# A quarter of the weights' low parts on GpSimd, in the mixers of the second block

## The chip, the cores and the metric

The kernel runs on one core of one Trainium2 chip. The metric is device time in microseconds, from the start of the program to its end. The engines are named as in the profile: PE is TensorE (PEld its weight loads), DVE is VectorE, ACT is ScalarE, POOL is GpSimd, SP is SyncE, whose queue issues the loads of weights.

## The reference

A sequence of 256 positions with 1024 features goes through two blocks. The first has four layers (attention of three kinds, each followed by a SwiGLU feed-forward). The second, where the change lies, has two layers of this form:

```
h = rmsnorm(x, attn_norm_g[layer])
proj = h @ w_in[layer]
gm_u, gm_v, ssm_z, ssm_xbc, ssm_dt, da_q, da_k, da_v, gates = split_cols(proj, IN_SIZES)
y_a = chunked_spatial_gating(gelu(gm_u), gelu(gm_v), ...)
y_b = mamba2_mixer(ssm_z, ssm_xbc, ssm_dt, ...)
y_c = diff_attention(da_q, da_k, da_v, ...)
g = sigmoid(gates).reshape(bsz, s, N_BRANCH, D_MODEL)
merged = (g[:, :, 0] * (y_a @ w_branch_a[layer]) + g[:, :, 1] * (y_b @ w_branch_b[layer])
          + g[:, :, 2] * (y_c @ w_branch_c[layer]))
x = x + merged @ w_out[layer]
h = rmsnorm(x, ffn_norm_g[layer])
up = causal_dwconv(h @ ffn_w_up[layer], ffn_conv_w[layer], ffn_conv_b[layer])
gate, val = split(up, 2, axis=-1)
x = x + (silu(gate) * val) @ ffn_w_down[layer]
```

The part up to `merged @ w_out` is the mixer. All of it is in float32.

## The kernel before

**Products in three parts.** A float32 product with weights is made from high and low parts. An operand is split into a high part (a cast to fp32r) and a low part (the operand minus its high part), and `mm3` adds three matmuls in one PSUM bank: high by high (L394), high by low weight (L395), low by high weight (L396). The sequence is two tiles of 128 positions, t = 0 and t = 1, each of which uses every weight.

**Weights in units and halves.** `plan` lists all weights as units in the order in which tile t = 0 uses them: first-block units, then, from `units_1` on, those of the second block. A unit is 4 rows of 128 by 512 columns, or 2 rows by 1024. It is loaded in two halves; half a of unit n has the number 2n + a. `load` makes a half: SP's queue loads it into a raw buffer (four of them, `wr`), ScalarE casts the high part into a buffer `w` (seven of them in the second block, `wh`) at L382, and then two subtractions of 128x512 (L385), one for each half of the columns, make the low part from the raw buffer and the high part. The raw buffer comes free when the second subtraction has ended, the `w` buffer when the matmuls of both tiles have read it. `get` asks for a half when tile t = 0 needs it and for one half ahead (`AHEAD = 1`).

**Who makes low parts.** The set `self.aside`, filled in `run`, holds the numbers of the halves whose low part GpSimd makes; VectorE makes all others. `part` gives every unit a kind: 0 for a mixer and 1 for a feed-forward of the first block, 2 for a mixer and 3 for a feed-forward of the second. Before the change the set holds 11 halves, just behind changes from one part to the next in the first block (`BOUND`); none lie in the second block.

**What sets the order.** The code issues the work of the two tiles in turns, tile t = 1 four turns behind (`LAG`), with tasks spawned for the convolution (L985 on VectorE, history copies L976 and L979 on GpSimd), state space (`ssm`, L1033 to L1104), differential attention (`diff_attn`), gates and merges (L1318 to L1325). The Tile framework then lays the order of the instructions of each engine when the kernel is built, after its own estimate of their durations, so that the matmuls of the two tiles interleave; each engine runs its own queue strictly in that order. Tiles named `pj`, `ch` and `tp` are PSUM banks, and so are the `accs` of L526 (`layer_norm`); all others lie in SBUF. Small loads, such as gains, are DMAs on GpSimd's queue (L494).

Of the kernel before, what the change touches and what calls it, by code (L numbers as in the profile page):

```python
# [82 lines left out]
class Net:  # L83
# [1338 lines left out]
    def run(self):  # L1422
        self.units = self.plan()
        self.index = {u[0]: n for n, u in enumerate(self.units)}

        self.aside = set()
        part = [2 * (n >= self.units_1) + ("ff" in str(u[0])) for n, u in enumerate(self.units)]
        for n in range(1, len(part)):
            if part[n - 1] != part[n]:
                self.aside |= {2 * n + a for a in BOUND[part[n]]}  # L1430
        self.loaded = 0
        self.tiles = {}
        self.cache = {}
        self.tasks = [[], []]
        self.x = []
        self.load_x()
        self.streams = [self.stream(0), self.stream(1)]
        self.live = [True, True]
        if not self.first:
            self.passed = 2  # L1440

        self.late = bool(self.first) and self.first[0] % 3 == 0
        n = 0
        while any(self.live):
            if self.live[0]:
                self.turn(0)
            if n == TABLES:
                self.tables()
                if not self.late:
                    for _ in self.more_tables():  # L1450
                        pass
            if self.live[1] and (n >= LAG or not self.live[0]):
                self.turn(1)
            n += 1
        self.phase.close()
# [29 lines left out]
```

## Time and profile before

| | us |
|---|---|
| median of 3 runs | 2401.51 (2400.18 to 2401.63) |
| the profiled execution | 2397.69 |
| its span, first to last instruction | 2395.8 |
| TensorE busy | 2358.1 |
| VectorE busy | 1739.8 |
| ScalarE busy | 1320.2 |
| GpSimd busy | 148.1 |

The granted TensorE clock is 0.999 of full speed over the span. In the profile's rows a time is in microseconds unless marked ns; L385 is line 385 of the kernel; `w<-raw,w` says what an instruction writes and reads; "xN" is a count. The first layer's mixer of the second block runs from about 1420 to 1700 us, the second layer's from about 1915 to 2195.

### The profile page before, as it was taken

The page shows a single profiled execution, that of the slowest core. Times are in us where ns is not written, and L with a number is a line of the kernel's source. Part 1 is how long each engine was busy: PE and PEld are TensorE (multiplying, and loading weights), DVE is VectorE, ACT ScalarE, POOL GpSimd, SP SyncE. Part 2 cuts the span into 40 slices and gives each one's busy share as a digit, 9 for nine tenths or more (in the row PEclk, how much of TensorE's full clock was granted, in tenths as well). Part 3 has the DMA queues.
Part 4 walks back from the last instruction along what each step waited for, and adds up shares of the span by engine and source line. Part 5 has one row for each costly group of instructions (what it writes and reads, how often), then busy time and mean ns, then how long its engine had stood idle before and what let it go on. Part 6 is the DMA issues. An engine that isn't in the chain of part 4 may idle for free.

```text
span 2395.8 us, 35093 instructions
## 1 busy us (share of the span) xinstructions
PE 2358.1 (98%) x11720; PEld 1926.0 (80%) x11720; DVE 1739.8 (73%) x4255; ACT 1320.2 (55%) x2182; POOL 148.1 (6%) x428
## 2 busy tenths in 40 slices
PE   8999999999999999999999999999999999999999
PEld 6788878888788788887778878887888788888887
DVE  7755576666755767557775588987877889987876
ACT  6544456555444555444544445744577656545776
POOL 1100000000100001000010000100011201000111
PEclk9999999999999999999999999999999999999999
DMA  6366654444566545665365657567565686575653
GB/s 233 106 189 189 185 167 132 133 132 131 171 189 187 185 132 167 187 188 184 124 182 190 186 140 168 136 147 198 165 194 184 166 187 132 123 213 172 189 184 115
DMA packets 280117, 400.16 MB, mean 167 GB/s; under 512 B 20588, under 2 KB 205098, under 8 KB 279936
## 3 DMA queue, kind: packets, MB, share of 16 engines
q1 hardware_dynamic: 274784, 381.88, 54.8%
q0 software_dynamic: 5152, 16.05, 2.2%
q8 instruction: 92, 1.51, 0.3%
q14 instruction: 89, 0.73, 0.1%
HBM read 396.81 MB, written 1.05 MB: 166 GB/s over the span
## 4 chain that ended last, share of the span: by engine, by line
PE 87%; DVE 8%; DMA 3%; ACT 2%; issue 1%; SPq 0%; ACTq 0%; DVEq 0%
PE pj L394 21%; PE pj L396 21%; PE pj L395 21%; PE tp L439 4%; PE ch L394 4%; PE ch L396 4%; PE ch L395 4%; PE ch L596 3%; PE ch L634 2%; DVE w L385 2%; DMA raw<-in_w_in_dram 2%; PE tp L646 1%; ACT w L382 1%; DMA raw<-in_a_w_qkv_dram 1%; DVE convy L985 1%
## 5 line engine op out<-in xcount | busy, mean ns | idle before, releaser
L385 DVE TENSOR_TENSOR w<-raw,w 128x512 fp32r<-128x512 f32 x1434 | 942.9, 684 | 469.3 <-ACT w L382 468.2
L382 ACT CAST w<-raw 128x1024 fp32r<-128x1024 f32 x728 | 758.5, 1043 | 661.2 <-PE pj L396 370.9
L394 PE MATMUL pj<-w,xth 128*128 128x512 f32 x2048 | 820.4, 401 | 7.1 <-ACT xth L432 6.8
L395 PE MATMUL pj<-w,xth 128*128 128x512 f32 x2048 | 803.3, 393 | 1.1 <-DVE w L385 1.1
L396 PE MATMUL pj<-w,xtl 128*128 128x512 f32 x2048 | 802.4, 393 | 1.8 <-DVE xtl L433 1.8
L394 PEld LDWEIGHTS pj<-w,xth 128*128 128x128 f32 x2048 | 385.5, 188 | 90.8 <-ACT xth L432 12.4
L396 PEld LDWEIGHTS pj<-w,xtl 128*128 128x128 f32 x2048 | 385.0, 188 | 86.4 <-DVE xtl L433 5.0
L395 PEld LDWEIGHTS pj<-w,xth 128*128 128x128 f32 x2048 | 386.0, 188 | 76.8 <-DVE w L385 2.0
L394 PE MATMUL ch<-w,fht 128*128 128x512 f32 x412 | 171.4, 416 | 1.8 <-ACT fht L432 1.8
L396 PE MATMUL ch<-w,fht 128*128 128x512 f32 x412 | 161.4, 392 | 0.0
L395 PE MATMUL ch<-w,fht 128*128 128x512 f32 x412 | 160.9, 391 | 0.0
L985 DVE SCALAR_TENSOR_TENSOR convy<-xc,ffn_cw,convy 128x128 f32<-128x128 f32 x352 | 100.7, 347 | 7.1 <-POOL ffn_hist L976 2.1
L396 PEld LDWEIGHTS ch<-w,fht 128*128 128x128 f32 x412 | 77.3, 188 | 17.9 <-DVE fht L433 1.0
L394 PEld LDWEIGHTS ch<-w,fht 128*128 128x128 f32 x412 | 77.5, 188 | 15.4 <-ACT fht L432 3.9
L395 PEld LDWEIGHTS ch<-w,fht 128*128 128x128 f32 x412 | 77.9, 189 | 11.9
L623 ACT ACTIVATE pexp<-ch,nm 128x128 f32<-128x128 f32 (+1 forms) x192 | 65.6, 421 | 33.8 <-DVE nm L618 24.0
L827 ACT ACTIVATE ffg<-pj 128x256 f32<-128x256 f32 x88 | 33.8, 384 | 86.2 <-PE pj L396 86.2
L982 ACT ACTIVATE convy<-xc,ffn_cw 128x128 f32<-128x128 f32 x176 | 72.8, 484 | 1.4
L634 PEld LDWEIGHTS ch<-v,pt 128*128 128x128 f32 x576 | 70.6, 192 | 2.9
L394 PE MATMUL pj<-w,fht 128*128 128x512 f32 x180 | 71.3, 396 | 0.0
L396 PE MATMUL pj<-w,fht 128*128 128x512 f32 x180 | 70.7, 393 | 0.0
L395 PE MATMUL pj<-w,fht 128*128 128x512 f32 x180 | 70.2, 390 | 0.0
(333 smaller groups left out, 2758.8 us busy)
## 6 DMA issues: line engine op xcount, KB each, us to landing
raw<-in_w_gate_up_dram SPq DMA_DIRECT2D x352, 256.0 KB, 3.2
raw<-in_w_in_dram SPq DMA_DIRECT2D x128, 512.0 KB, 5.1
raw<-in_w_down_dram SPq DMA_DIRECT2D x88, 512.0 KB, 3.6
raw<-in_ffn_w_up_dram SPq DMA_DIRECT2D x176, 256.0 KB, 3.3
raw<-in_b_w_qkv_dram SPq DMA_DIRECT2D x144, 256.0 KB, 3.1
raw<-in_ffn_w_down_dram SPq DMA_DIRECT2D x44, 512.0 KB, 4.4
raw<-in_a_w_qkv_dram SPq DMA_DIRECT2D x24, 512.0 KB, 4.4
raw<-in_c_w_qkv_dram SPq DMA_DIRECT2D x48, 256.0 KB, 3.2
```

The source lines that it names most:

```text
L382: nc.scalar.copy(w[:, 0, :m], raw)
L385: e.tensor_sub(w[:, 1, s], raw[:, s], w[:, 0, s].bitcast(F32))
L394: mm(ps, xh[:, k, :], wh[:, kk, cols], start=start, stop=False)
L395: mm(ps, xh[:, k, :], wl[:, kk, cols], start=False, stop=False)
L396: mm(ps, xl[:, k, :], wh[:, kk, cols], start=False, stop=stop)
L439: self.nc.tensor.transpose(tp[:, b * P:(b + 1) * P], src[:, b * P:(b + 1) * P], self.ident)
L596: nc.tensor.matmul(svs[par][:, a, j * P:(j + 1) * P], q(par, a), k(par, a, j), start=True, stop=True)
L623: nc.scalar.activation(p[:, a, :(t + 1) * P], sv[:, a, :], AF.Exp, bias=n2[:, a:a + 1])
L634: nc.tensor.matmul(o[:, par + 2 * a, :], pts[par][:, a * (t + 1) + j, :], v(j, par + 2 * a), start=j == 0, stop=j == t)
L827: nc.scalar.activation(g, ps[:, :FFC], AF.Silu)
L982: nc.scalar.activation(y[:, a, :], xc[:, a, 4:], AF.Identity, bias=b[:, 0, c:c + 1], scale=w[:, h, c:c + 1])
L985: nc.vector.scalar_tensor_tensor(y[:, a, :], xc[:, a, o:o + P], w[:, j, c:c + 1], y[:, a, :], op0=OP.mult, op1=OP.add)
```

## The change

One statement is added in `run`: in the mixers of the second block (kind 2), the first half of each unit with an even number goes into the set of halves whose low part GpSimd makes. Each mixer has 45 units, from number 208 and from number 286, so these are 46 halves of 180. Each is two subtractions of 128x512. The unit of the time steps (`dt`, 16 columns) has an odd number and stays as it is. Nothing else in the code changes: `load` picks the engine, `e`, by the set.

```
--- before.py
+++ after.py
@@ -1428,6 +1428,8 @@
         for n in range(1, len(part)):
             if part[n - 1] != part[n]:
                 self.aside |= {2 * n + a for a in BOUND[part[n]]}
+
+        self.aside |= {2 * n for n in range(len(part)) if part[n] == 2 and n % 2 == 0}
         self.loaded = 0
         self.tiles = {}
         self.cache = {}
```

## Rows read from the trace of the kernel before

**Rows 1.** The page, first part: busy time, share of the span, instructions.

```profile
PE 2358.1 (98%) x11720; PEld 1926.0 (80%) x11720; DVE 1739.8 (73%) x4255; ACT 1320.2 (55%) x2182; POOL 148.1 (6%) x428
```

**Rows 2.** Table by stretches: length; busy PE, PEld, DVE, ACT, POOL; clock, DMA share, GB/s.

```profile
1480.00:1550.00 70.00, 69.82 (x395) 57.27 (x392) 67.02 (x211) 49.63 (x104) 8.70 (x26) 1.00 0.59 144
1550.00:1645.00 95.00, 93.35 (x481) 76.53 (x479) 83.40 (x205) 44.29 (x63) 1.74 (x4) 1.00 0.65 152
...
1980.00:2045.00 65.00, 64.75 (x364) 53.51 (x364) 61.28 (x199) 46.58 (x95) 10.88 (x27) 1.00 0.57 128
2045.00:2140.00 95.00, 94.53 (x490) 78.53 (x489) 85.23 (x201) 45.05 (x62) 1.09 (x2) 1.00 0.67 160
...
sum 543.00, PE 537.65 PEld 441.13 DVE 462.23 ACT 295.58 POOL 25.66; mean PE 67.21 PEld 55.14 DVE 57.78 ACT 36.95 POOL 3.21
```

**Rows 3.** Waits of PE, 1426 to 1700: releaser, us in total, times, longest.

```profile
PE pj L394 <- DVE sg L1318: 1.5, 1, 1.5
PE pj L395 <- DVE w L385: 1.1, 1, 1.1
```

**Rows 4.** Waits of SP's DMA queue, 1426 to 1700.

```profile
SPq L374 <- DVE w L385: 244.4, 84, 8.7
```

**Rows 5.** Groups, count, busy us and mean ns: VectorE 1420 to 1700, GpSimd whole.

```profile
L385 DVE TENSOR_TENSOR w<-raw,w 128x512 fp32r<-128x512 f32 (+1 forms) x169 | 110.4, 673 | 20.6 <-ACT w L382 20.4
...
L385 POOL TENSOR_TENSOR w<-raw,w 128x512 fp32r<-128x512 f32 x22 | 28.6, 1319 | 556.8 <-ACT w L382 547.0 <-DVE eg L789 9.8
```

**Rows 6.** Timeline, ACT and DVE near 1668: start, us, instruction, [idle before].

```profile
1667.41 1.05 ACT L382 CAST w<-raw 128x1024 fp32r<-128x1024 f32 x1 [1.67 <-issue]
...
1668.76 1.29 DVE L385 TENSOR_TENSOR w<-raw,w 128x512 fp32r<-128x512 f32 x2
```

**Rows 7.** Timeline, POOL's subtractions near 923 and 1111 and DVE under them.

```profile
923.34 2.60 POOL L385 TENSOR_TENSOR w<-raw,w 128x512 fp32r<-128x512 f32 x2 [1.04 <-ACT w L382]
...
923.49 1.24 DVE L473 SCALAR_TENSOR_TENSOR rs_a<-rs_y,bnve 128x1 f32<-128x1 f32 x1
...
1111.68 2.56 POOL L385 TENSOR_TENSOR w<-raw,w 128x512 fp32r<-128x512 f32 x2 [164.41 <-ACT w L382]
...
1111.86 0.69 DVE L526 SCALAR_TENSOR_TENSOR x<-x,ch 128x512 f32<-128x512 f32 x1 [0.46 <-PE ch L396]
```

**Rows 8.** Lines 473 and 477: duration ns min/median/max, first and last start.

```profile
L473 DVE SCALAR_TENSOR_TENSOR rs_a<-rs_y,bnve x48: 182/213/1254, 104.4 to 1418.7; 128x1 f32<-128x1 f32 x48
...
L477 DVE SCALAR_TENSOR_TENSOR rs_y<-rs_a,rs_y x96: 143/158/1219, 104.9 to 2020.9; 128x1 f32<-128x1 f32 x60, 128x8 f32<-128x8 f32 x24, 128x4 f32<-128x4 f32 x12
```

**Rows 9.** Timeline of DVE: first and last of fourteen lengthened instructions.

```profile
106.13 0.73 DVE L477 SCALAR_TENSOR_TENSOR rs_y<-rs_a,rs_y 128x1 f32<-128x1 f32 x1
...
1211.79 1.00 DVE L473 SCALAR_TENSOR_TENSOR rs_a<-rs_y,bnve 128x1 f32<-128x1 f32 x1
```

**Rows 10.** Groups of DVE, 1420 to 1700: the convolution.

```profile
L985 DVE SCALAR_TENSOR_TENSOR convy<-xc,ssm_cw,convy 128x128 f32<-128x128 f32 x72 | 20.1, 347 | 0.6 <-issue 0.5
```

**Rows 11.** Timeline, ACT, DVE and PE, 1552 to 1566: one half's cast, subtraction, use.

```profile
1552.42 1.05 ACT L382 CAST w<-raw 128x1024 fp32r<-128x1024 f32 x1
...
1554.83 2.71 DVE L985 SCALAR_TENSOR_TENSOR convy<-xc,ssm_cw,convy 128x128 f32<-128x128 f32 x10
...
1565.05 0.68 DVE L385 TENSOR_TENSOR w<-raw,w 128x512 fp32r<-128x512 f32 x1
...
1565.95 0.40 PE L395 MATMUL pj<-w,xth 128*128 128x512 f32 x1
```

**Rows 12.** Timeline, ACT and PE, 1635 to 1639: a half's cast and first use.

```profile
1635.27 1.05 ACT L382 CAST w<-raw 128x1024 fp32r<-128x1024 f32 x1 [2.31 <-PE tp L439]
...
1638.19 0.48 PE L394 MATMUL pj<-w,xth 128*128 128x512 f32 x1
```

**Rows 13.** Timeline of POOL, 1545 to 1604.

```profile
1545.67 2.13 POOL L979 COPY xc<-ssm_hist 128x3 f32<-128x3 f32 x4 [4.68 <-DVE spa L1000]
...
1603.38 0.56 POOL L494 DMA_DIRECT2D sng<-in_ssm_norm_g_dram  x1 [51.31 <-DVE ssl L1085]
```

More of the change, by code (lines that the diff above doesn't have):

```diff
@@ L1430, in run @@
                 self.aside |= {2 * n + a for a in BOUND[part[n]]}
+        self.aside |= {2 * n for n in range(len(part)) if part[n] == 2 and n % 2 == 0}
         self.loaded = 0
```

## The prediction

> **What bounds the kernel now.** I read the page first: TensorE is busy 98% of the span, VectorE 73%, ScalarE 55%, GpSimd 6% [rows 1]. An edit that takes work from VectorE can therefore win only where TensorE waits for it. The edit acts in the two mixers of the second block, so the second view was the table by stretches: in the 543 us from 1426 to 1700 and from 1926 to 2195, TensorE is busy 537.65 us and VectorE 462.23 us (85%), by the last row, which sums all eight stretches [rows 2]. TensorE stands still for only 543 - 537.65 = 5.4 us there; since a matmul's end is modelled, some more waiting hides in lengthened matmuls. The stages are unlike. In the four stretches 1480:1550, 1550:1645, 1980:2045 and 2045:2140 (convolution, state space, attention; 325 us, "dense" below) VectorE is idle 3.0 + 11.6 + 3.7 + 9.8 = 28 us; in the other four it is idle 543 - 462 - 28 = 53 of 218 us. The view of waits names what TensorE waits for in the first mixer: the low part of a weight (1.1 us) and the merge of a branch (1.5 us), both VectorE's [rows 3]. VectorE also holds up the loads: the DMA queue waits 244.4 of 274 us for a low part, because the subtraction is the last reader of a raw buffer, and there are four of those [rows 4]. So the edit has a point; the question is what GpSimd's work does to VectorE.
>
> **The change part by part.** Each mixer has 45 units and starts at an even unit number (208 and 286), so even units are 23 in each: 46 first halves, two subtractions each, 92 instructions move.
>
> *Off VectorE.* One subtraction lasts 0.67 us [rows 5], but two in a row take 1.29 us together, so each occupies the engine 1.29 - 0.69 = 0.60 us [rows 6]. 92 x 0.60 = 55 us come off the 462.
>
> *Onto GpSimd.* The 22 that it makes now last 1.319 us each [rows 5]: 92 x 1.32 = 121 us on an engine that is busy 25.7 us in those 543 [rows 2]. It does not become a bound.
>
> *What GpSimd's instruction costs VectorE.* This decides the sign. Under GpSimd's subtractions at 923.34, VectorE's little L473 takes 1.24 us [rows 7], where its group's median is 0.213 [rows 8]; it ends when the first subtraction ends. Under those at 1111.68, VectorE's L526 of 128x512 takes its plain 0.69 us [rows 7]. The difference is where the inputs lie: L473 reads two tensors from SBUF, L526 reads one from SBUF and one from PSUM (accs). I went through all of VectorE's instructions that overlap one of the 22: fourteen are longer than the median of their group, from L477 at 106.13 to L473 at 1211.79 [rows 9], all fourteen read two SBUF tensors, and together they are 9.35 us longer. That is 9.35 / 22 = 0.42 us of lost VectorE time per GpSimd subtraction, the lower bound; the upper bound is its whole duration, 1.32 us. The Trainium skill (SBUF — State Buffer, section "Who interferes with whom") says that a VectorE instruction with two SBUF inputs contends with a GpSimd instruction that reads SBUF, and that whoever comes first at the shared ports keeps them for its whole instruction while the other stands still. By that rule alone, with VectorE always at the port, the whole 1.32 us would be lost each time, which the second rival prices; the trace agrees with the mechanism and shows a third of that price so far.
>
> Where those 22 ran, VectorE was mostly in a layer norm on PSUM operands or waiting. The mixers differ: the subtractions themselves and the convolution's L985 make up 110.4 + 20.1 us of VectorE's time in one mixer, which is about 462 / 2 = 231 [rows 2, 5, 10], and they read two SBUF tensors each, as do the norms, gates and rope. So I went to the end of each of the 46 casts, where GpSimd could start, left out the half's own two subtractions, and read how much of its 1.25 us is left when VectorE next begins an instruction with two SBUF inputs. One example of each kind: the cast that starts at 1552.42 ends at 1553.47 amid the convolution, whose ten L985 follow in one run of 2.71 us, so both subtractions would block in full [rows 11]; the one that starts at 1667.41 ends at 1668.46, and VectorE's next work is the very two subtractions that leave it, so next to nothing is blocked [rows 6]. The sum over the 46 is 57 us, 0.62 each, between the bounds. I take it. Over both mixers VectorE thus gains 55 and loses 57: nothing. But it is split unevenly: in the dense stretches 22 halves free 44 x 0.60 = 26 us and block 34 us, a net loss of 8 us; the quiet ones gain 6 us where VectorE idles anyway, worth nothing.
>
> *From VectorE to TensorE.* In the dense stretches TensorE follows VectorE closely: the low part finished by the subtraction that starts at 1565.05 is read at 1565.95 [rows 11]. Of the 8 us I let half through, since VectorE still has 28 us of idle time there: +4 us (bounds 0 and 8).
>
> *What the moved halves gain.* They leave VectorE's queue. The half cast by 1553.47 gets its low part begun only at 1565.05 [rows 11]; GpSimd would have it done near 1556.5, and its raw buffer would be free that much earlier, for one load in four. That can shorten the two waits of [rows 3]: I take -1.5 us in all (bounds 0 and -5.4, TensorE's idle time).
>
> *Is GpSimd too slow?* It needs 0.08 + 2 x 1.3 = 2.6 us from the cast's end to the second piece. The moved half with the least time is cast from 1635.27 to 1636.32 and first used at 1638.19 [rows 12], with its second piece due at 1639.2, 2.9 us after the cast. One lock wait would make it late by under 1 us. The other 45 have 2.8 to 18 us. I take 0 (bounds 0 and 2).
>
> *Other queues.* No DMA is added; SP's loads keep their order. On GpSimd's queue the subtractions stand among copies of the convolution's history, which start VectorE's convolution [rows 13], and DMAs of gains that wait for a free slot. A copy behind a pair of subtractions comes up to 2.6 us late; covered by VectorE's backlog, taken as 0 (bounds 0 and 3). The Tile framework also lays a new order of instructions on all engines when the kernel is built; nothing in the trace prices that, and I allow 3 us to either side, about the sum of the two waits of [rows 3].
>
> Sum: 4 - 1.5 = +2.5 us. The profiled execution took 2397.7 us (2395.8 of span), so 2400.2 by it; the runs shown have a median of 2401.5, 3.8 more, so 2404.
>
> **The rivals.**
> *VectorE is relieved (faster).* If the block stays at the 0.42 us of [rows 9], the dense stretches gain 44 x (0.60 - 0.42) = 8 us of VectorE time, and the loads run ahead. TensorE then gets back its 5.4 us of idle time and a little of what hides in lengthened matmuls: about -7, 2394.5. For it speaks that VectorE holds the loads [rows 4]; against it, that the mixers hold far more two-input work than the places of the 22.
> *The lock takes VectorE (slower).* In the dense stretches VectorE always has another two-input instruction next. At 1.0 us per subtraction it loses 44 x 0.40 = 18 us there, and of its 28 idle us many are waits for TensorE's scores and products, so two thirds go through: +12, 2413.5. At the whole 1.32 us it would be 32 us lost, past all idle time, and about +20. It decides from about 0.85 us per instruction, where the loss in the dense stretches passes 11 us and about 5 of it gets through. For it: the convolution run in [rows 11]. Against: 0.78 is what the reading gives for the dense stretches.
> *A stopped GpSimd queue (slower).* The gain's DMA at 1603.38 sat 51.31 us waiting for VectorE to free its slot [rows 13]. Were the half cast by 1553.47 queued behind it, its low part, due at 1565.95, would come some 38 us late: 2440. It needs Tile to have ordered the two the wrong way round.
> *It does less than it says.* If gain and loss both fall into slack, the time stays 2401.5; that lies within the forecast.
>
> **How the numbers follow.** The forecast, no change that can be told, has 0.41, and by itself 2397 to 2406.5; relief 0.24; the lock 0.31; the stopped queue 0.04. A measurement of this kernel can tell about 0.2% (4.8 us) from no change, so faster is 0.24, same 0.41, slower 0.35. The range takes in the relief and the lock at 1.0 us with 1 us around each: 2393 to 2415; outside it are the stopped queue, the lock at its full price and a gain beyond TensorE's idle time.
>
> **What would show it.** Right: 92 more GpSimd subtractions of 1.25 to 1.6 us, VectorE's two-input instructions under them lengthened by about 0.6 us each, VectorE's busy time in the mixers about where it was, TensorE's busy share there within a percent. Relief: TensorE's idle time in the dense stretches near zero and the DMA queue's wait for low parts clearly below 244 us. The lock: VectorE's dense stretches above 95%, and new waits of TensorE for low parts, scores and merges. Wrong altogether: TensorE waiting for GpSimd's own low parts for more than 2 us, or a change of time outside the two mixers.

## The result

The changed kernel takes 2426.28 us (median of 5 runs, 2424.43 to 2428.62) against 2401.51: the ratio is 1.0108, interval 1.0096 to 1.0119. It is slower by 24.8 us, outside the predicted range and on the side to which I gave 0.35. The profiled execution took 2425.71 us, 2424.0 of it span, 28.2 more than before.

The first part of the page of the changed kernel (busy time, share of the span, instructions) answers to [rows 1]:

```profile
PE 2365.8 (98%) x11720; PEld 1929.3 (80%) x11720; DVE 1742.9 (72%) x4163; ACT 1319.7 (54%) x2182; POOL 271.1 (11%) x520
```

GpSimd has its 92 subtractions more. VectorE has 92 fewer and yet is busy 3.1 us longer: what it was relieved of it lost again, as predicted. The table by stretches, columns as in [rows 2], shows where the time went (the work stands some microseconds later than before in the same stretch):

```profile
1480.00:1550.00 70.00, 64.93 (x355) 52.06 (x356) 64.02 (x184) 40.10 (x88) 16.64 (x26) 0.98 0.51 115
1550.00:1645.00 95.00, 88.65 (x465) 72.35 (x464) 88.32 (x203) 48.25 (x74) 23.07 (x23) 1.00 0.63 148
...
1980.00:2045.00 65.00, 60.08 (x325) 47.99 (x324) 59.78 (x176) 38.12 (x80) 14.98 (x22) 1.00 0.57 121
2045.00:2140.00 95.00, 90.60 (x479) 75.17 (x478) 84.78 (x207) 49.94 (x80) 22.47 (x30) 0.96 0.59 145
...
sum 543.00, PE 520.51 PEld 423.89 DVE 453.60 ACT 284.15 POOL 132.53; mean PE 65.06 PEld 52.99 DVE 56.70 ACT 35.52 POOL 16.57
```

In the four dense stretches TensorE stood still 0.2 + 1.7 + 0.2 + 0.5 = 2.6 us before [rows 2]; now it is 5.1 + 6.4 + 4.9 + 4.4 = 20.7 us. VectorE's idle time in the same stretches is 6.0 + 6.7 + 5.2 + 10.2 = 28.1 us, and it was 28 before. So TensorE waits more while VectorE has no less to spare: no engine is full, and what is lost is lost in waits of one engine for another.

Waits of PE in the changed kernel (releaser: us in total, times, longest), first from 1426 to 1700, where [rows 3] stood, then from 1980 to 2140, where two waits of 0.3 and 0.2 us stood:

```profile
PE tp L439 <- DVE stg L566: 4.0, 2, 3.0
PE tp L439 <- DVE convy L1227: 2.6, 1, 2.6
PE pj L395 <- DVE w L385: 2.1, 2, 1.4
PE tp L646 <- DVE dap L1137: 1.2, 2, 0.7
...
PE ch L1043 <- DVE ssda L1033: 3.4, 1, 3.4
PE tp L646 <- DVE dap L1137: 2.6, 3, 1.7
PE tp L439 <- DVE rs_a L476: 2.2, 1, 2.2
```

Hardly any of it is for low parts (2.1 us). TensorE waits for the ends of VectorE's chains: the norm and rope of queries and keys (L476, L566), the convolution (L1227), the attention's softmax (L1137), softplus (L1033). The first of these can be followed instruction by instruction. The timeline of the changed kernel, GpSimd, VectorE and TensorE:

```profile
1476.56 2.56 POOL L385 TENSOR_TENSOR w<-raw,w 128x512 fp32r<-128x512 f32 x2 [3.27 <-ACT w L382]
...
1476.53 1.35 DVE L476 TENSOR_TENSOR rs_a<-rs_a,rs_y 128x8 f32<-128x8 f32 x2
...
1477.87 1.35 DVE L477 SCALAR_TENSOR_TENSOR rs_y<-rs_a,rs_y 128x8 f32<-128x8 f32 x2
...
1482.48 0.28 DVE L566 TENSOR_TENSOR stg<-ropea,ropeb 128x128 f32<-128x128 f32 x1
...
1482.91 0.63 PE L439 MATMUL tp<-ident,stg 128*128 128x128 f32 x4 [3.04 <-DVE stg L566]
```

and the same two pairs of instructions in the kernel before:

```profile
1473.27 0.28 DVE L476 TENSOR_TENSOR rs_a<-rs_a,rs_y 128x8 f32<-128x8 f32 x2
...
1473.54 0.24 DVE L477 SCALAR_TENSOR_TENSOR rs_y<-rs_a,rs_y 128x8 f32<-128x8 f32 x2
```

Each row is a pair, and in each pair one tiny VectorE instruction is held until one of GpSimd's two subtractions ends: 1.35 instead of 0.28 us, 1.35 instead of 0.24. These are links of the chain that ends at L566, and TensorE, which runs its queue strictly in order, stands 3.04 us in front of the transpose that reads it. In the kernel before it stood 0.78 us in front of these transposes already:

```profile
1478.03 0.63 PE L439 MATMUL tp<-ident,stg 128*128 128x128 f32 x4 [0.78 <-DVE stg L566]
```

The two holds, 1.07 and 1.11 us, are about the rest. A stop of that length costs a second time. The table by stretches around it (the third figure from the right is the granted clock):

```profile
1479.00:1483.00 4.00, 0.96 (x5) 0.49 (x4) 4.00 (x17) 0.88 (x2) 0.12 (x1) 1.00 0.59 189
1483.00:1487.00 4.00, 4.00 (x20) 2.92 (x21) 2.63 (x8) 0.73 (x2) 0.00 (x0) 0.58 0.27 77
1487.00:1491.00 4.00, 4.00 (x21) 3.13 (x20) 3.34 (x12) 4.00 (x13) 0.00 (x0) 0.99 0.17 61
```

After TensorE stood nearly still for 3 us, the granted clock is 0.58 over the next 4 us, so for most of them at the lower level of 1.2 GHz, the 1.7 us that 0.42 x 4 makes. Over the page TensorE's busy time is 7.7 us longer, 2365.8 after 2358.1; the other 20 of the 28 us are standing still.

Two rows on the moved work itself: the group of GpSimd's subtractions, with the 22 old ones (answers to [rows 5]), and the waits of SP's queue from 1426 to 1700 (answers to [rows 4]):

```profile
L385 POOL TENSOR_TENSOR w<-raw,w 128x512 fp32r<-128x512 f32 x114 | 158.0, 1405 | 1048.9 <-ACT w L382 1012.4 <-DVE ropeb L565 10.1 <-DVE eg L789 9.8
```

```profile
SPq L374 <- DVE w L385: 158.8, 56, 12.2
SPq L374 <- POOL w L385: 49.5, 18, 4.2
SPq L374 <- ACT w L382: 25.4, 17, 4.6
```

The 92 last (158.0 - 28.6) / 92 = 1.41 us each, and no row of TensorE's waits names a low part of GpSimd. The loads wait less for low parts, 208 against 244 us, but as much more for other work: for ScalarE's casts it is 25.4 us, where 3.7 stood before, and the queue's waits are 251 us in all, after 250. The loads did not run ahead.

### The profile page after: what moved, and what is told of

The parts are those of the page before. It is cut to its first block, busy times and chain, and to the rows that moved or that the text cites. A ratio compares the mean times of both kernels' runs of the same rounds, so it can differ in the third digit from the quotient of the medians.

```text
span 2424.0 us, 35135 instructions
## 1 busy us (share of the span) xinstructions
PE 2365.8 (98%) x11720; PEld 1929.3 (80%) x11720; DVE 1742.9 (72%) x4163; ACT 1319.7 (54%) x2182; POOL 271.1 (11%) x520
## 4 chain that ended last, share of the span: by engine, by line
PE 83%; DVE 11%; ACT 2%; issue 2%; DMA 2%; POOL 0%; ACTq 0%; SPq 0%; DVEq 0%; POOLq 0%
PE pj L394 20%; PE pj L396 20%; PE pj L395 20%; PE ch L394 4%; PE ch L396 4%; PE tp L439 4%; PE ch L395 4%; PE ch L596 2%; PE ch L634 2%; DVE w L385 2%; DVE convy L985 2%; PE tp L646 1%; DMA raw<-in_a_w_qkv_dram 1%; ACT w L382 1%; PE ch L1092 1%
## 5 line engine op out<-in xcount | busy, mean ns | idle before, releaser
L385 DVE TENSOR_TENSOR w<-raw,w 128x512 fp32r<-128x512 f32 (+1 forms) x1342 | 889.4, 689 | 484.6 <-ACT w L382 483.5
L385 POOL TENSOR_TENSOR w<-raw,w 128x512 fp32r<-128x512 f32 x114 | 158.0, 1405 | 1048.9 <-ACT w L382 1012.4
L623 ACT ACTIVATE pexp<-ch,nm 128x128 f32<-128x128 f32 (+1 forms) x192 | 65.6, 421 | 33.7 <-DVE nm L618 23.9
L439 PE MATMUL tp<-ident,stg 128*128 128x128 f32 x416 | 67.8, 277 | 7.5 <-DVE stg L566 4.4
L394 PE MATMUL pj<-w,fht 128*128 128x512 f32 x180 | 71.2, 395 | 0.0
```

The source lines that it names most:

```text
L385: e.tensor_sub(w[:, 1, s], raw[:, s], w[:, 0, s].bitcast(F32))
L394: mm(ps, xh[:, k, :], wh[:, kk, cols], start=start, stop=False)
L439: self.nc.tensor.transpose(tp[:, b * P:(b + 1) * P], src[:, b * P:(b + 1) * P], self.ident)
L623: nc.scalar.activation(p[:, a, :(t + 1) * P], sv[:, a, :], AF.Exp, bias=n2[:, a:a + 1])
```

## The experiments

In each text, "lock" or "hold" is GpSimd's subtraction keeping a VectorE instruction from starting or ending; "relief" is the 92 subtractions that leave VectorE; "order" is the order of instructions that the Tile framework lays. Differences are medians against the kernel before, run beside it on the same chip. Where VectorE's time is given, it is the busy time of the page, 1739.8 us before.

### Hold or order

*lock_alone.* The line of the change fills another set, `extra`, and GpSimd subtracts the high part `w[:, 0]` from itself, beside VectorE. `scratch` is one tile in which the four attention masks of the kernel before were laid together:

```
-        self.aside |= {2 * n for n in range(len(part)) if part[n] == 2 and n % 2 == 0}
+        self.extra = {2 * n for n in range(len(part)) if part[n] == 2 and n % 2 == 0}
...
+        for s in (slice(0, m // 2), slice(m // 2, m)) if 2 * i + a in self.extra else ():
+            nc.gpsimd.tensor_sub(self.scratch.bitcast(F32), w[:, 0, s].bitcast(F32), w[:, 0, s].bitcast(F32))
```

> Part varied: VectorE keeps all 92 subtractions, so the kernel before is left whole and its instruction order is nearly kept (39 lines of difference on TensorE against 3951 in the changed kernel). GpSimd only gets an extra 128x512 subtraction per quarter at the same 46 halves, of the bf16-rounded part from itself into an idle tile, whose result nobody uses. Theory 'lock' (GpSimd's subtractions hold back VectorE's short instructions, in chains whose end TensorE waits for): the loss comes without the move, at least 24 us and up to 45, as VectorE has no relief here; 2426 to 2446 us, with VectorE instructions lengthened by some 50 us in all. Theory 'order' (the instruction order that came with the move costs the time): 2401 to 2405 us.

Measured: 2423.28 us, +23.4, ratio 1.0102 (1.0085 to 1.0119), 3 us under the range for a lock. The page, part 1:

```profile
PE 2366.6 (98%) x11720; PEld 1928.4 (80%) x11720; DVE 1791.3 (74%) x4255; ACT 1320.2 (55%) x2182; POOL 271.2 (11%) x520
```

VectorE is busy 51.5 us longer with the same instructions, 0.56 per added subtraction. The largest wait in its dense stretches, on the timeline of GpSimd, VectorE and TensorE:

```profile
2063.11 2.69 POOL L387 TENSOR_TENSOR masks<-w 128x512 f32<-128x512 f32 x2 [2.08 <-ACT w L382]
...
2063.62 1.01 DVE L1004 SCALAR_TENSOR_TENSOR spz<-spq,spz 128x16 f32<-128x16 f32 x1
2064.55 0.34 DVE L985 SCALAR_TENSOR_TENSOR convy<-xc,ssm_cw,convy 128x128 f32<-128x128 f32 x1
2064.82 1.01 DVE L1006 SCALAR_TENSOR_TENSOR ssdt<-spz,ssdt 128x16 f32<-128x16 f32 x1
...
2068.94 0.40 PE L1043 MATMUL ch<-ssda,triu 128*128 128x16 f32 x1 [2.85 <-DVE ssda L1033]
```

Two links of softplus take 1.01 us each, where the kernel before has 0.17 for each, and TensorE waits 2.85 us for the product L1033 that follows from them, where it had no such wait before. The hold alone makes the loss: TensorE's and ScalarE's order is that of the kernel before, and VectorE's nearly so.

*fill_alone.* The same with `nc.gpsimd.memset(self.scratch.bitcast(F32), 0.0)` as GpSimd's instruction.

> As lock_alone, but the 92 extra GpSimd instructions fill the idle tile with zeros instead of subtracting: they write 128x512 and read nothing. Theory 'lock by two-operand reads': 2401 to 2404 us, no VectorE instruction lengthened. If any GpSimd instruction that touches the buffer for a microsecond holds VectorE back: as lock_alone in kind, 2410 to 2430 us. Theory 'order': 2401 to 2405 us.

Measured: 2401.26 us, +1.4, ratio 1.0007 (0.9998 to 1.0017); VectorE 1739.9 us. No instruction with two SBUF inputs is lengthened under a fill. Seven small TENSOR_SCALAR instructions with one input are, by 0.14 to 0.46 us and 1.9 us together:

```profile
1540.46 0.63 DVE L997 TENSOR_SCALAR spz<-spa 128x16 f32<-128x16 f32 x1
```

This one takes 0.17 us in the kernel before. Nothing of it is seen in the time, and the queue traffic of 92 more instructions costs nothing. (In these two kernels the tile's zeros unmask the second block's attention; *lock_idle_tile*, below, does without that.)

*order_no_lock.*

```
-            e.tensor_sub(w[:, 1, s], raw[:, s], w[:, 0, s].bitcast(F32))
+            nc.gpsimd.memset(w[:, 1, s].bitcast(F32), 0.0) if 2 * i + a in self.extra else e.tensor_sub(w[:, 1, s], raw[:, s], w[:, 0, s].bitcast(F32))
```

> The changed kernel with its order of instructions kept on TensorE, VectorE and ScalarE line by line, but at the 46 moved halves GpSimd fills the low parts with zeros instead of subtracting: the low parts of these halves are left out of the result. VectorE is relieved as in the change and GpSimd reads nothing. Theory 'lock': no loss, 2394 to 2403 us (relief without its price). Theory 'order': the loss stays, 2420 to 2427 us.

Measured: 2395.36 us, -4.6, ratio 0.9980 (0.9971 to 0.9989), VectorE 1692.6 us. With the changed kernel's own order and without the reads the loss is gone. (A fill waits for neither the load nor the cast, and the raw buffer is free after the cast; so this run and *relief_old_order* below may gain a little more than relief alone.)

*short_pieces.*

```
-        for s in (slice(0, m // 2), slice(m // 2, m)):
+        for s in [slice(b, b + m // 4) for b in range(0, m, m // 4)] if 2 * i + a in self.aside and i >= self.units_1 else (slice(0, m // 2), slice(m // 2, m)):
```

> The changed kernel with each of the 92 moved subtractions cut in two of 128x256, so GpSimd does the same work in 184 instructions of about 0.7 us each; order on TensorE, VectorE and ScalarE as in the change. Theory 'lock', held for the length of one GpSimd instruction: a VectorE instruction waits for half as long, and a chain gets through between two pieces: the loss is about half, 2410 to 2418 us. If instead the loss goes with the total time that GpSimd holds, or with the order: 2424 to 2430 us.

Measured: 2423.20 us, +23.3, ratio 1.0094 (1.0079 to 1.0109). The half that I expected of a hold of half the length did not come. Counted as in the prediction, over all VectorE instructions longer than the median of their group by over 0.1 us and less the 10.4 us that the kernel before has, the holds are 44 us here against 50 in the changed kernel. Beyond the 18 that are long in the kernel before, 96 instructions are held for 0.46 us on the mean, against 58 for 0.86. The pieces themselves last 0.85 us, not half of 1.41.

### What else holds, and place or amount

*copy_alone.* `nc.gpsimd.tensor_copy(self.scratch.bitcast(F32), w[:, 0, s].bitcast(F32))`, with the mask that the second block reads in a tile of its own.

> As lock_alone, but GpSimd's 92 extra instructions copy the rounded part (one operand read, one written, 128x512) into an idle tile that nothing reads. If only an instruction that reads two operands holds VectorE back: 2399 to 2404 us with no VectorE instruction lengthened. If any GpSimd read does: 2415 to 2425 us, and VectorE's busy time goes up by 40 us or more.

Measured: 2411.54 us, +11.3, ratio 1.0045 (1.0030 to 1.0060); VectorE 1762.7 us. Neither expectation was met: one read operand holds too, but only 22.9 / 92 = 0.25 us a time, at 0.94 us an instruction. The Trainium skill (SBUF — State Buffer, "Who interferes with whom") says that a VectorE instruction with two SBUF inputs contends with a GpSimd instruction that reads SBUF and not with one that only writes it. By that, the copy holds such instructions and the fill doesn't: both runs agree.

*move_in_chains* and *move_elsewhere* split the change by place:

```
+        self.aside |= {2 * n for n in range(len(part)) if part[n] == 2 and n % 2 == 0 and 10 <= (n - self.units_1) % 78 <= 26}
...
+        self.aside |= {2 * n for n in range(len(part)) if part[n] == 2 and n % 2 == 0 and not 10 <= (n - self.units_1) % 78 <= 26}
```

> The real move, but only for 18 of the 46 halves (per mixer the units 10 to 26, even): those whose GpSimd subtractions ran, in the changed kernel, between 1464 and 1590 and between 1968 and 2071 us, where TensorE waited for ends of VectorE's chains. 36 subtractions on GpSimd, so some 20 us of VectorE time held. Theory 'place' (a hold costs where a short VectorE instruction stands in a chain that TensorE is about to need, and nothing elsewhere): nearly the whole loss, 2416 to 2428 us. Theory 'amount' (the loss goes with the sum of holds): 18/46 of it, 2408 to 2412 us.

> The complement of move_in_chains: the other 28 of the 46 halves are moved, 56 subtractions on GpSimd, some 30 us of VectorE time held. Theory 'place': 2399 to 2404 us. Theory 'amount': 28/46 of the loss, 2413 to 2418 us.

Measured: 2420.44 us, +20.2, ratio 1.0085 (1.0068 to 1.0101), for the 36 subtractions near the chains; 2412.30, +12.1, ratio 1.0050 (1.0035 to 1.0065), for the 56 others. The first is as "place" wants it, the second nearly as "amount" does, and together they make 32 us, more than the whole change. Per subtraction the chains are the dearer place, but no place is free; what makes them dearer is looked at below, with the order kept.

*vector_extra.* `nc.vector.tensor_sub` of 480 columns into the idle tile, at the same halves.

> GpSimd gets nothing new; VectorE keeps all low parts and does 92 further subtractions of 128x480 into an idle tile at the same 46 halves, some 0.56 us each, 52 us in all, as much as the holds took in lock_alone (VectorE busy 1739.8 to 1791.3 us). Unlike a hold, this work stands in the program, and the instruction order is laid with it (4299 lines of difference on TensorE against the kernel before). Theory 'VectorE time is what counts, whatever takes it': 2418 to 2430 us. Theory 'a hold is worse than work, as it falls on chain instructions and the order is laid without it': 2401 to 2412 us.

Measured: 2416.29 us, +16.1, ratio 1.0066 (1.0050 to 1.0082); VectorE 1786.8 us. Between the two expectations: 47 us of plain VectorE work cost 16, less than as many us of holds, and far from nothing.

*move_odd_units.* `n % 2 == 1`, without the unit of the time steps.

> The same change with the first half of every odd unit of the mixers in place of the even ones (as many halves but one or two). If the loss belongs to such a move in general: 2415 to 2430 us. If it is an accident of which halves the even ones are: 2400 to 2410 us.

Measured: 2435.63 us, +34.3, ratio 1.0142 (1.0127 to 1.0157). These are 42 halves, 84 subtractions. The loss belongs to such a move in general, and is larger here than I had expected of any. The holds, counted as for *short_pieces*, are 47 us, so a held us costs 0.73 us, against 0.50 in the change: which halves move matters too, and no run shows why.

### With the order kept

In the kernels of this part but *order_alone* and *lock_idle_tile*, TensorE's, VectorE's and ScalarE's instructions are pinned to the order of the kernel before, by edges that order the issue and add no wait for an end. The list of names is kept in the kernel; line numbers are 4 or 5 higher there.

```
+        keep_order(nc, tc)
...
+        names = [k for k in names if by[k].engine != by["I-90"].engine]
+        for a, b in zip(names, names[1:]):
+            tc.add_manual_dep(by[b], a, mybir.DependencyInfo(mybir.DependencyClass.NoSync, mybir.DependencyReason.DATA), reason="order")
```

> The change itself (46 halves on GpSimd), but the instructions of TensorE, VectorE and ScalarE are pinned to the order that they have in the kernel before; only the 92 subtractions leave VectorE's queue. So VectorE has the relief (some 55 us) and the holds (some 50 us), and no new order. Theory 'order spends the relief' (the new order puts chains and the transposes that read them earlier, as if VectorE were free, and the holds then strike there): 2400 to 2408 us. Theory 'relief does not reach the chains' (the low parts that leave had slack; a hold delays whatever short instruction stands next): 2417 to 2428 us.

Measured: 2425.15 us, +23.9, ratio 1.0097 (1.0082 to 1.0113). The loss comes whole without the new order.

> The kernel before with TensorE's and ScalarE's instructions pinned to the order of the changed kernel (656 of TensorE's 10904 matmuls and transposes stand at another place); VectorE makes all low parts, GpSimd gets nothing new. If the new order by itself costs time: 2410 us or more. If it doesn't: 2397 to 2406 us.

Measured: 2415.90 us, +14.6, ratio 1.0058 (1.0043 to 1.0073). The new order, which was laid for a relieved VectorE, costs a VectorE that is not relieved 14.6 us. VectorE's own order is not pinned in this run, and is neither that of the kernel before nor that of the changed one; it may have a part in the 14.6.

*lock_idle_tile* is *lock_alone* with the mask of the second block in a tile of its own. Nothing is pinned in it; TensorE's and ScalarE's order is that of the kernel before all the same.

> lock_alone again with an output tile that nothing else reads or writes in the second block (in lock_alone and fill_alone the tile also held a mask of the attention, so the mask was zero there and GpSimd's instructions stood in a dependence with VectorE's reads of it). If the shared tile had no part in the loss: 2419 to 2428 us with VectorE's busy time near 1791 us. If it had: under 2412 us.

Measured: 2429.35 us, +28.1, ratio 1.0111 (1.0094 to 1.0128); VectorE 1796.4 us, a little more of both than expected. The shared tile had no part in the loss.

*relief_old_order* has the zero fill of *order_no_lock*, pinned.

> move_old_order, but GpSimd fills the 46 halves' low parts with zeros instead of subtracting: the low parts of these halves are left out of the result. VectorE has the relief and no holds, in the order of the kernel before. Theory 'the low parts that leave had slack': 2395 to 2402 us, so that the holds in move_old_order cost 23 us or more. If the relief were worth in the old order what the prediction counted and move_old_order had a further cost of its own: under 2392 us.

Measured: 2392.10 us, -8.1, ratio 0.9966 (0.9953 to 0.9979), between the two expectations, 0.1 us above the second. The page, part 1:

```profile
PE 2355.7 (98%) x11720; PEld 1926.7 (81%) x11720; DVE 1688.4 (71%) x4163; ACT 1319.4 (55%) x2182; POOL 186.5 (8%) x520
```

51.4 us less for VectorE bring 8.1 us.

*extra_old_order* is *vector_extra* with each extra subtraction pinned right behind the low part of its half.

> vector_extra with the order pinned to that of the kernel before; each of the 92 extra VectorE subtractions (128x480, some 0.56 us) stands right behind the low part of its half, GpSimd gets nothing new. The same amount of VectorE time as the holds of lock_idle_tile (+28 us), at other places. Theory 'any VectorE time added in these stretches is as dear': 2418 to 2430 us. Theory 'a hold is dear because it falls on chain instructions': 2403 to 2414 us.

Measured: 2416.55 us, +16.3, ratio 1.0069 (1.0052 to 1.0086), between the two again. The page, part 1:

```profile
PE 2364.0 (98%) x11720; PEld 1925.3 (80%) x11720; DVE 1788.7 (74%) x4347; ACT 1320.5 (55%) x2182; POOL 151.3 (6%) x428
```

> move_in_chains (18 halves, 36 subtractions on GpSimd) with the order of the kernel before. Theory 'place': 2414 to 2424 us. Theory 'amount': 36/92 of the loss of move_old_order (23.9 us), 2409 to 2412 us.

> move_elsewhere (28 halves, 56 subtractions on GpSimd) with the order of the kernel before. Theory 'place': 2401 to 2409 us. Theory 'amount': 56/92 of 23.9 us, 2414 to 2417 us.

Measured: 2415.01 us, +14.8, ratio 1.0065 (1.0050 to 1.0080), and 2412.18, +11.9, ratio 1.0048 (1.0033 to 1.0063). That is 14.8 / 36 = 0.41 us per subtraction near the chains and 11.9 / 56 = 0.21 elsewhere. The pages, part 1:

```profile
PE 2363.4 (98%) x11720; PEld 1929.5 (80%) x11720; DVE 1747.7 (72%) x4219; ACT 1319.5 (55%) x2182; POOL 195.8 (8%) x464
PE 2366.4 (98%) x11720; PEld 1929.9 (80%) x11720; DVE 1731.9 (72%) x4199; ACT 1320.9 (55%) x2182; POOL 228.0 (9%) x484
```

A subtraction that leaves relieves VectorE of 51.4 / 92 = 0.56 us, so 20.1 and 31.3 us here. The holds are then 1747.7 - 1739.8 + 20.1 = 28.0 us and 1731.9 - 1739.8 + 31.3 = 23.4 us, or 0.78 and 0.42 us per subtraction. Per us of hold the loss is 0.53 and 0.51 us: the same. Place doubles the price of a subtraction because it about doubles the hold; that a held us costs more near a chain than elsewhere is not shown. "Amount" is right if the amount is that of the holds and not of the subtractions.

Put side by side, what one us of VectorE's time is worth to the whole:

| run | VectorE busy, change | time, change | per us |
|---|---|---|---|
| relief, old order | -51.4 | -8.1 | 0.16 |
| relief, new order | -47.2 | -4.6 | 0.10 |
| work added, old order | +48.9 | +16.3 | 0.33 |
| holds by copies | +22.9 | +11.3 | 0.49 |
| holds by subtractions, *lock_alone* | +51.5 | +23.4 | 0.45 |
| holds by subtractions, *lock_idle_tile* | +56.6 | +28.1 | 0.50 |
| the change, old order | +0.5 | +23.9 | |

The intervals of the times leave 0.26 to 0.42 for added work, 0.40 to 0.55 for holds by subtractions and 0.31 to 0.63 for holds by copies. So the gap between work and holds is likely, and not sure; that to relief is sure.

## Why the prediction was wrong

**Right: the mechanism and its size.** *Off VectorE*, 55 us: the runs with a fill show 51.4 and 47.2. *Onto GpSimd*, 1.32 us each: 1.41, within the 1.25 to 1.6 named. *What GpSimd's instruction costs VectorE*, 0.62 us, between 0.42 and 1.32: 50 / 92 = 0.54 by lengthened instructions in the changed kernel, 0.56 by busy time in *lock_alone*. So the net for VectorE was about nothing, as forecast (+3.1 us on the page, +0.5 in the old order). The Trainium skill's rule (SBUF — State Buffer, "SBUF: two separate sides") that whichever starts first has the shared ports for its whole instruction fits the two pairs at 1476.53. The mean of 0.54 is 0.38 of the 1.41 us that a subtraction lasts.

**Wrong: the step "From VectorE to TensorE".** It offset relief against holds, kept a net loss of 8 us for the dense stretches, and let half of that through: +4. The net itself was about right: in the dense stretches of the changed kernel 42 subtractions left, 23.5 us at 0.56 each, and the holds are 29.4 us. But the runs price the two apart: at most 0.16 us per us of relief, 0.45 to 0.50 per us of hold. Half was about right, but for the whole 50 us of holds, in the quiet stretches too, and not for a net. With the measured rates the step would have been 50 x 0.45 to 0.50, less 8, which is +14 to +17; measured are 23.9 in the old order and 24.8 in the new.

Why a us given back is not worth a us taken is in part argued. A low part that leaves was seldom what TensorE waited for: 1.1 us in the first mixer [rows 3]. A hold falls on whatever VectorE has next: of the 76 lengthened instructions of the changed kernel 11 are low parts, of the 101 of *lock_idle_tile*, where VectorE keeps all its subtractions, 42. Some are links of a chain that TensorE is about to read, as at 1476.53. But *lock_idle_tile* pays 0.50 per us with so many low parts among the held, and the two places above pay 0.53 and 0.51; so that the chains make the price is not shown. The 7 to 10 us between the sum of the rates and the change stay open, and so does why a us of hold seems to cost more than a us of added work (0.33).

**The premise behind it.** I read VectorE's 28 us of idle time in the dense stretches as room [rows 2]. It was waiting for other engines' results: before, some 17 of the 28 us end with a result of ScalarE and 9 with one of TensorE; in the changed kernel it is 13 and 13. Of VectorE's waits from 1480 to 1645 in the kernel before, the second to the fourth:

```profile
DVE ssl L1088 <- ACT ssl L1087: 3.0, 3, 1.8
DVE w L385 <- ACT w L382: 2.2, 3, 1.4
DVE ssl L1085 <- PE ch L1081: 2.1, 4, 0.9
```

The changed kernel has the same 28 us of idle time and 18 us more of TensorE standing still. That the engines' waits form a loop, each waiting for what its own result starts, is the likely reading; it is not followed round here. For the same reason my sign for the lock, "VectorE's dense stretches above 95%", never showed (91, 93, 92 and 89%), while the loss came all the same.

**The rivals.** *The lock takes VectorE* was the right side, with the mechanism, but I let it decide only from 0.85 us per subtraction; it decided at 0.54. Its 2413.5 at 1.0 us was too low by the same mistake. *VectorE is relieved* named -7 for a relief of 8 us in the dense stretches; the runs without holds give -4.6 and -8.1 for the whole relief. *A stopped GpSimd queue* did not come: TensorE never waits for GpSimd's low part.

**The small terms.** *What the moved halves gain*, -1.5: not seen; TensorE's waits for low parts went from 1.1 to 2.1 us in the first mixer, and the loads wait as long as before. *Is GpSimd too slow*, 0: right. *Other queues* and the new order, within 3 us: right for the change (24.8 against 23.9 with the old order), by luck, since that order costs 14.6 in *order_alone*, without the relief for which it was laid. The clock was not in the prediction at all. How much of TensorE's 7.7 us of longer busy time is its share stays open: *extra_old_order* has 5.9 us of it with a mean clock of 0.999 over the span, as before, where the changed kernel has 0.996.

## What to carry to other kernels

Price work taken from an engine and delay put on it apart, each where it falls: relief counts only where another engine waits for that very work, and a delay can strike anything that an in-order engine is about to read. Count the delay in us held and not in instructions moved: near the chains a subtraction held twice as much as elsewhere, and cost twice as much. Idle time of the second engine is no room where it waits for the others' results; before counting on it, look at what ends each idle piece. GpSimd is a place for element-wise work that reads SBUF only where VectorE's two-input instructions have slack; here two pairs of tiny instructions, 0.28 and 0.24 us long and each held once, took TensorE's wait from 0.8 to 3 us.

## What the runs showed of the hardware

A GpSimd copy of 128x512 (0.94 us, one read operand) holds VectorE by 0.25 us on the mean, a subtraction (1.35 to 1.41 us) by 0.54 to 0.62, and a fill (0.53 us) holds no instruction with two SBUF inputs, but lengthened seven TENSOR_SCALAR instructions with one, by 0.14 to 0.46 us. Cutting the subtraction in two did not lower the price: 184 instructions with 44 us of holds cost 23.3 us, 92 with 50 us cost 24.8. A stop of TensorE of 3 us was followed by about 4 us at a granted clock of 0.58.
